# Feed-forward gate and up tiles as a 2x2 block product with seven products

## The chip, the cores and the metric

The kernel is one program on one core of a Trainium2 chip. Its time is device microseconds (us). Four engines compute: TensorE (PE; its weight loads are listed as PEld), VectorE (DVE), ScalarE (ACT) and GpSimd (POOL). SyncE (SP) issues all DMA transfers from one queue, in order. Every engine takes its own instructions in the order in which they stand in the program, and waits for others through semaphores.

## The reference, cut to what matters

The reference is an encoder of two layers (DEPTH = 2) on one sequence of 512 tokens of 1024 features, in float32. In each layer four token mixers (retention, chunk attention, gated linear attention and S5, a diagonal state-space model) work on projections of x. Their outputs are gated and summed, projected by `w_out` and normalised. A SwiGLU feed-forward part follows:

```python
x = _layer_norm(DEEPNORM_ALPHA * x + mixed @ w_out[l], ln1_g[l], ln1_b[l])
ffn = (jax.nn.silu(x @ w_ffn_gate[l]) * (x @ w_ffn_up[l])) @ w_ffn_down[l]
x = _layer_norm(DEEPNORM_ALPHA * x + ffn, ln2_g[l], ln2_b[l])
```

`w_ffn_gate` and `w_ffn_up` are 1024 x 2816, `w_ffn_down` is 2816 x 1024; 2816 is 22 tiles of 128.

## The kernel before, in words

All large products are made in a split form. An operand is cut into a high part that TensorE takes exactly and the low rest, and each product is three matmuls: high by high, low by high, high by low (`three`). A weight tile comes from DRAM as `wr` (128 x 1024, that is 8 blocks of 128 x 128 along the 1024 features); ACT casts it to `wh`, DVE subtracts that to `wl`. x is kept transposed in `XH` and `XL`.

A layer goes through four stages. (1) The mixers, a long stretch of small pieces that a planner (`Pace`, `run`) puts in order. (2) The `w_out` projection: `proj_ln` adds up 8 k-tiles in eight PSUM banks (`pj`), four token tiles t of 128 tokens by two halves of 512 features, then normalises each token tile (`layer_norm`). Its `rest` transposes the token tile (`tp`), scales it and writes it split into `XH` and `XL`; its `rows` scales it in rows, with 16 GpSimd operations in all, for the residual of the next projection. (3) Gate and up: for each of the 22 tiles f, two products `pg` (gate, then up) of 128 features by 512 tokens, each 8 blocks by 3 matmuls of 512 columns; ACT takes the silu, DVE multiplies to `fs`, and `fs` is split into `gh` and `gl` for the last stage. The first three products are made in two token halves of 256 columns (`gemm_ts`), so that TensorE has work while the token tiles t = 2 and 3 are normalised. (4) The down projection: `proj_ln` with 22 k-tiles of 24 matmuls. The first 18 go in the order of k, the last four by token tile.

One more thing runs beside stage 3 of layer 0, on GpSimd and DVE: the S5 constants of layer 1 (`s5_constants(1)`, tiles `s5w`, `ea`, `eb`), and from them eight tables (`s5_table`, tiles `er`, `ei`, `et`), which are stored in DRAM (`esp`) for the mixers of layer 1:

```python
if l + 1 < L and f == 0:
    s5c = s5_constants(l + 1)
if l + 1 < L and f % 2 == 0 and 4 <= f < 20:
    j = f // 2 - 2
    for i, x in enumerate(s5_table(j, s5c[3])):
        SP.dma_start(esp[j, i], x)
```

The order within an engine is the order of emission, moved by a scheduler that follows what is due. Tiles live in pools of 2 KB slots (53 general ones, 7 for `sg`, 8 for `acc`); a new tile waits until all that read or wrote its slot's last tile are done. The names in `order` and in the trace are the tile names; numbers behind them are single buffers.

Of the kernel before, what the change touches and what calls it, by code (L numbers as in the profile page):

```python
# [38 lines left out]
# 2 KB slots of SBUF per partition: in general, gates on hold, sums over branches  # L39
BUFS = {"a": 53, "sg": 7, "acc": 8}  # L40
# [92 lines left out]
def trunk_kernel(ctx: ExitStack, tc: tile.TileContext, xn, xt, wt, w2, wbr, wo, wgu, wdn,  # L133
# [12 lines left out]
    ap_ = pool("ap", 53)  # L146
# [9 lines left out]

    def slot(s, dt=F32, tag="a"):
        n = nm(s)
        return ap_.tile([P, 512], dt, tag=tag, name=n, bufs=BUFS[tag])

# [20 lines left out]

    def three(pairs):
# [44 lines left out]
        # theta * 2^k, reduced by multiples of 2 pi (exact products of short parts)  # L227
# [39 lines left out]
        # powers of exp(i theta), by doubling  # L267
# [22 lines left out]
    def s5_table(j, tabs):  # L290
        """exp(i theta n), n = 0..511, of a state tile"""
# [13 lines left out]
    # ------------------------------------------------------------- weight streams  # L305
# [17 lines left out]
    def wload_s(src):  # L323
        """the same into slots, in halves"""
# [10 lines left out]
    def gemm_t(src, s, late=None):  # L335
        """[128 features, 512 tokens] = (weight tile)^T x^T, in PSUM"""
# [17 lines left out]
    def gemm_n(srcs, width, pre=None, late=None):  # L354
        """four [128 tokens, width] = x (weight columns), in PSUM"""
# [24 lines left out]
    # ---------------------------------------------------------------- layer norm  # L380
    def layer_norm(l, w_, xh, pss, gt, bt, t, last):
        """x = LN(ALPHA x + psum) of one token tile, in place, the scale and shift left
        out; returns what is to be emitted later: x^T, split, and the scale and shift in rows"""
# [9 lines left out]
        power = G.tensor_tensor(rs, ve, mhalf, ALU.pow)  # L393
# [44 lines left out]
        return rest, rows, power  # L438

    def proj_ln(l, w_, lh, ll, nk, wsrc, kl, ks, xh, gt, bt, last):  # L440
        """x = LN(ALPHA x + a w): a^T split in lh/ll (nk k-tiles), w streamed by rows;
        returns what is left to do for the last token tile"""
# [20 lines left out]
        for t in range(4):  # L463
# [3 lines left out]
            todo.append(layer_norm(l, w_, xh[t], pss[t], gt, bt, t, last))  # L467
            if t > 0 and not last:
                todo[t - 1][0]()

        def rows():
            with tc.issue_after(todo[3][2].ins):
                for x in todo:
                    x[1]()

        return todo[3][0], rows
# [758 lines left out]
```

## Time and profile before

| | before |
|---|---|
| median of 3 runs | 1728.72 us (1725.3, 1728.72, 1729.99) |
| span of the profiled execution | 1727.3 us |
| TensorE busy, of the span | 1667.3 us, 97% |
| VectorE / ScalarE / GpSimd busy | 1000.5 / 621.2 / 347.6 us |
| gate and up, layer 0 (501.5 to 754.1) | 252.6 us |
| down projection, layer 0 (754.1 to 878.0) | 123.9 us |
| gate and up, layer 1 (1345 to 1600) | 255.0 us |

The profile is of one execution; the page gives its span, 1727.3 us, and no other time of that execution, which lies 1.4 us under the median of the runs. A stage's row in the view by windows gives the length of the window and then each engine's busy time and instructions. TensorE's records overlap (a matmul's end is modelled), so how fast it goes is read from the distance of the starts.

### The profile page before, as it was taken

The page shows a single profiled execution, that of the slowest core. Times are in us where ns is not written, and L with a number is a line of the kernel's source. Part 1 is how long each engine was busy: PE and PEld are TensorE (multiplying, and loading weights), DVE is VectorE, ACT ScalarE, POOL GpSimd, SP SyncE. Part 2 cuts the span into 40 slices and gives each one's busy share as a digit, 9 for nine tenths or more (in the row PEclk, how much of TensorE's full clock was granted, in tenths as well). Part 3 has the DMA queues.
Part 4 walks back from the last instruction along what each step waited for, and adds up shares of the span by engine and source line. Part 5 has one row for each costly group of instructions (what it writes and reads, how often), then busy time and mean ns, then how long its engine had stood idle before and what let it go on. Part 6 is the DMA issues. An engine that isn't in the chain of part 4 may idle for free. (4 is left out here: it accounts for less than half of the span.)

```text
span 1727.3 us, 19511 instructions
## 1 busy us (share of the span) xinstructions
PE 1667.3 (97%) x7468; PEld 1348.2 (78%) x7468; DVE 1000.5 (58%) x1473; ACT 621.2 (36%) x1012; POOL 347.6 (20%) x363
## 2 busy tenths in 40 slices
PE   8999998889999999999999999999999999999997
PEld 6778786667887888888887788877778888888886
DVE  4667579888577533322374765799875733333225
ACT  4454542233343322221253545433343532222112
POOL 0601025550038921000051000122200600000002
PEclk9998999899999999999999999999999999999999
DMA  6532212222423333322316433133424323322322
GB/s 198 174 108 77 85 61 93 81 88 91 145 94 98 122 122 122 110 98 97 110 61 235 130 99 95 62 119 122 135 80 158 104 92 98 98 87 97 98 98 73
DMA packets 66173, 186.41 MB, mean 108 GB/s; under 512 B 7136, under 2 KB 7328, under 8 KB 66080
## 3 DMA queue, kind: packets, MB, share of 16 engines
q1 hardware_dynamic: 66080, 185.17, 32.8%
q8 instruction: 59, 0.97, 0.2%
q14 instruction: 34, 0.28, 0.0%
HBM read 170.46 MB, written 14.68 MB: 107 GB/s over the span
## 5 line engine op out<-in xcount | busy, mean ns | idle before, releaser
L121 DVE TENSOR_TENSOR wl<-wr,wh 128x1024 fp32r<-128x1024 f32 (+2 forms) x250 | 316.8, 1268 | 537.3 <-PE pg L121 267.7
L121 ACT CAST wh<-wr 128x1024 fp32r<-128x1024 f32 (+2 forms) x250 | 257.5, 1031 | 554.2 <-PE pg L121 240.7
L121 PE MATMUL pg<-XH,wh 128*128 128x512 f32 (+1 forms) x1264 | 316.0, 391 | 1.8 <-DVE fs L121 1.8
L121 PE MATMUL pg<-XL,wh 128*128 128x512 f32 (+1 forms) x1264 | 314.1, 389 | 2.5 <-DVE XL L121 2.5
L121 PE MATMUL pg<-XH,wl 128*128 128x512 f32 (+1 forms) x1264 | 311.2, 388 | 0.0
L121 PEld LDWEIGHTS pg<-XL,wh 128*128 128x128 f32 x1264 | 233.1, 189 | 57.1 <-DVE XL L121 3.3
L121 PEld LDWEIGHTS pg<-XH,wh 128*128 128x128 f32 x1264 | 232.4, 190 | 55.6 <-issue 3.0
L121 PEld LDWEIGHTS pg<-XH,wl 128*128 128x128 f32 x1264 | 232.7, 189 | 54.0
L121 POOL TENSOR_TENSOR rs<-ve,ct 128x1 f32<-128x1 f32 x16 | 10.9, 682 | 727.5 <-DVE ve L121 727.5
L121 PE MATMUL pj<-wl,gh 128*128 128x512 f32 x320 | 102.9, 395 | 0.0
L121 PE MATMUL pj<-wh,gh 128*128 128x512 f32 x320 | 102.7, 394 | 0.0
L121 PE MATMUL pj<-wh,gl 128*128 128x512 f32 x320 | 102.6, 394 | 0.0
L121 POOL TENSOR_TENSOR acc<-acc,sg 128x512 f32<-128x512 f32 x32 | 55.3, 1732 | 170.6 <-DVE sg L121 170.6
L121 ACT CAST gh<-fs 128x512 fp32r<-128x512 f32 x44 | 27.3, 621 | 126.0 <-DVE fs L121 126.0
L121 PEld LDWEIGHTS pj<-wh,gh 128*128 128x128 f32 x320 | 60.3, 188 | 13.8
L121 PEld LDWEIGHTS pj<-wl,gh 128*128 128x128 f32 x320 | 60.3, 188 | 13.7
L121 PEld LDWEIGHTS pj<-wh,gl 128*128 128x128 f32 x320 | 60.3, 188 | 13.4
L121 PE MATMUL gn<-wh,XH 128*128 128x400 f32 (+1 forms) x128 | 49.8, 389 | 5.7 <-ACT XH L121 5.7
L121 ACT ACTIVATE sg<-pg,hb 128x512 f32<-128x512 f32 x64 | 43.9, 686 | 23.4 <-PE pg L121 23.1
L121 DVE TENSOR_TENSOR gl<-fs,gh 128x512 fp32r<-128x512 f32 x44 | 35.1, 797 | 29.7 <-ACT gh L121 29.7
L121 POOL TENSOR_TENSOR hr<-hv,ct 128x8 f32<-128x8 f32 x8 | 13.5, 1687 | 189.6 <-DVE hv L121 189.6
L121 PE MATMUL pb<-brh,bwh 128*128 128x512 f32 x128 | 51.6, 403 | 0.0
(320 smaller groups left out, 2562.2 us busy)
## 6 DMA issues: line engine op xcount, KB each, us to landing
wr<-in_wt SPq DMA_DIRECT2D x90, 512.0 KB
wr<-in_wgu SPq DMA_DIRECT2D x88, 512.0 KB
wr<-in_wdn SPq DMA_DIRECT2D x44, 512.0 KB
bwr<-in_wbr SPq DMA_DIRECT2D x32, 256.0 KB
wr<-in_wo SPq DMA_DIRECT2D x16, 512.0 KB
skr<-spr SPq DMA_DIRECT2D x32, 192.0 KB
wr<-in_w2b SPq DMA_DIRECT2D x8, 400.0 KB
wr<-in_w2a SPq DMA_DIRECT2D x8, 256.0 KB
```

What stands on the lines that cost most here:

```text
L121: r = fn(out, *a, **kw)
```

## The change

Per tile f, gate and up are now one 2 x 2 block product. The two block rows are gate and up; the inner dimension is cut into features 0-511 and 512-1023 (`a11, a12` of the gate's weights, `a21, a22` of up's), and the tokens into 0-255 and 256-511 (`b11, b21`, `b12, b22`). Seven block products stand for eight, each 4 blocks x 3 matmuls of 256 columns. They need sums of weights (`s1` to `s4`, four GpSimd additions of 128 x 512 per tile, each then split by ACT and DVE like a weight), sums of x blocks (`t1` to `t4`, made once per layer in `block_sums`), and five additions from PSUM on DVE per tile. The weight loads of gate (`wr`) and up (`wu`) stay two DMAs per tile.

Around it: `fs` times `fy` (`g`) is kept unsplit until the down projection, which splits it itself (`aph`, `apl`). The normalised rows are stored in DRAM (`xsp`) in `rest`, loaded again in `residual`, and scaled there by the 16 GpSimd operations that `rows` had, ahead of the next projection. SBUF's general slots are laid out anew for each phase: 37 + 7 + 8 for the mixers and the `w_out` projection, then 22 held tiles `g` with the feed-forward's own slots, then 30 for the down projection. The S5 constants and tables of layer 1 are emitted in the k loop of layer 0's down projection.

```diff
+MIXERS = {"a": 37, "sg": 7, "acc": 8}
+HELD = {"g": 22}
+FFN = {"wu": 2, "ws": 5, "wk": 14, "po": 7}
+DOWN = {"a": 30}
...
+    def block_sums(sums, t, xf):
+        raw, parts = sums
+        raw.append(xf)
+        if t < 2:
+            return
+        e = G if t == 2 else V
+        (b11, b21), (b12, b22) = raw[t - 2], xf
+        t1, t2, t3, t4 = (slot("bs", tag="a" if t == 2 else "g") for _ in range(4))
+        cols = slice(P * (t - 2), P * (t - 2) + P)
+        for i, (o, a, b) in enumerate(((t1, b12, b11), (t2, b22, t1), (t3, b22, b12), (t4, b21, t2))):
+            e.tensor_tensor(o, a, b, ALU.subtract)
+            h, l_ = (x[:, :, cols] for x in parts[i])
+            split(h, l_, o.rearrange("p (k c) -> p k c", c=P))
+
+    def residual(l, which, src, scaled):
+        xh = [[kept(f"x{h}") if t == 3 else slot("x") for h in range(2)] for t in range(4)]
+        gb = None if scaled else ln_params(l, which)
+        for t in range(4):
             for h in range(2):
-                G.tensor_tensor(xh[h], xh[h], gt[h], ALU.mult)
-                G.tensor_tensor(xh[h], xh[h], bt[h], ALU.add)
...
+                SP.dma_start(xh[t][h], src[P * t:P * t + P, 512 * h:512 * h + 512])
+                if gb:
+                    G.tensor_tensor(xh[t][h], xh[t][h], gb[0][h], ALU.mult)
+                    G.tensor_tensor(xh[t][h], xh[t][h], gb[1][h], ALU.add)
+        return xh
...
         for k in range(nk):
             ws[k] = (wload_s(wsrc[k]) if k >= nk - ks else
                      [halved(x) for x in wload(wsrc[k])])
+            if not isinstance(a[k], tuple):
+                a[k] = split_slots("ap", a[k])
+            if also:
+                also(k)
...
+        def weights(f):
+            rg, ru = wp.tile([P, 1024], F32, tag="wr", name=nm("wr"), bufs=2), slot("wu", tag="wu")
+            h, l_ = (wp.tile([P, 1024], F32R, tag=t, name=nm(t)) for t in ("wh", "wl"))
+            SP.dma_start(rg, wgu[l, 2 * f])
+            SP.dma_start(ru, wgu[l, 2 * f + 1])
+            split(h, l_, rg)
+            a11, a12, a21, a22 = rg[:, 0:512], rg[:, 512:1024], ru[:, 0:512], ru[:, 512:1024]
+            w = {1: (h[:, 0:512], l_[:, 0:512]), 2: (h[:, 512:1024], l_[:, 512:1024])}
+            s1, s2, s3, s4 = (slot("ws", tag="ws") for _ in range(4))
+            G.tensor_tensor(s1, a21, a22, ALU.add)
+            G.tensor_tensor(s2, s1, a11, ALU.subtract)
+            G.tensor_tensor(s3, a11, a21, ALU.subtract)
+            G.tensor_tensor(s4, a12, s2, ALU.subtract)
+            for n, x in ((6, s2), (5, s1), (7, s3), (3, s4), (4, a22)):
+                w[n] = split_slots("wk", x, ("wk", "wk"))
+            return w
...
+        def tile_of(w, pa, u, s):
+            pb, pc = mx_ps("fb")[:, 0:256], mm_ps("fc")[:, 0:256]
+            y = slot("fy", tag="po")
+            p1, u2, p15 = u[:, 0:256], u[:, 256:512], y[:, 256:512]
+            product(pb, w[6], t2, True)
+            V.tensor_tensor(u2, pb, p1, ALU.add)
+            product(pc, w[5], t1, True)
+            V.tensor_tensor(p15, pc, p1, ALU.add)
+            if s is None:
+                s = head2(w, pa)
+            product(pb, w[7], t3, False)
+            V.tensor_tensor(p15, pb, p15, ALU.add)
+            product(pc, w[3], b22, False)
+            V.tensor_tensor(s[:, 256:512], pc, u2, ALU.add)
+            A.activation(s[:, 256:512], s[:, 256:512], AF.Silu)
+            product(pb, w[4], t4, False)
+            V.tensor_tensor(y[:, 0:256], pb, p1, ALU.add)
+            return s, y
...
+    def tables(k):
+        if k == 0:
+            s5c_[0] = s5_constants(1)
+        elif k % 2 == 0 and k <= 16:
+            for i, x in enumerate(s5_table(k // 2 - 1, s5c_[0][3])):
+                SP.dma_start(esp[k // 2 - 1, i], x)
...
+        phase("ff", FFN)
+        gs = ffn(l, parts, rest)
+        close()
+        phase("dn", DOWN)
+        xh = residual(l, 0, xsp, False)
+        gt, bt = ln_params(l, 1) if l == L - 1 else (None, None)
+        rest = proj_ln(l, 1, gs, NF, wdn[l], 4, 2, xh, gt, bt, l == L - 1,
+                       also=tables if l + 1 < L else None)
```

Here is how this stands in the queues at three places. First TensorE at the entry of layer 0's gate and up, before the change; `tp` are the transposes of token tile 2 (`x_3916`, `x_3917`) and 3 (`x_3918`, `x_3919`):

```order
1057 L121 MATMUL tp_4292<-ct,x_3916 128x128 x4
1058 L121 MATMUL tp_4293<-ct,x_3917 128x128 x4
1059 L121 MATMUL pg_4342<-XH,wh_4325 128x256 x8
1060 L121 MATMUL pg_4342<-XL,wh_4325 128x256 x8
1061 L121 MATMUL pg_4342<-XH,wl_4326 128x256 x8
1062 L121 MATMUL pg_4343<-XH,wh_4331 128x256 x8
1063 L121 MATMUL pg_4343<-XL,wh_4331 128x256 x8
1064 L121 MATMUL pg_4343<-XH,wl_4332 128x256 x8
1065 L121 MATMUL tp_4393<-ct,x_3918 128x128 x4
1066 L121 MATMUL tp_4394<-ct,x_3919 128x128 x4
1067 L121 MATMUL pg_4344<-XH,wh_4337 128x256 x8
```

The same place after the change; `fa` are the block products of the gate's own weights, `fc_4577` is the first product with a weight sum (`wkh_4361` is the high part of `s1`):

```order
1035 L126 MATMUL tp_4296<-ct,x_3916 128x128 x4
1036 L126 MATMUL tp_4297<-ct,x_3917 128x128 x4
1037 L126 MATMUL fa_4377<-XH,wh_4343 128x256 x4
1038 L126 MATMUL fa_4377<-XL,wh_4343 128x256 x4
1039 L126 MATMUL fa_4377<-XH,wl_4344 128x256 x4
1040 L126 MATMUL tp_4394<-ct,x_3918 128x128 x4
1041 L126 MATMUL tp_4395<-ct,x_3919 128x128 x4
1042 L126 MATMUL fa_4468<-XH,wh_4434 128x256 x4
1043 L126 MATMUL fa_4468<-XL,wh_4434 128x256 x4
1044 L126 MATMUL fa_4468<-XH,wl_4435 128x256 x4
1045 L126 MATMUL fa_4377<-XH,wh_4343 128x256 x4
1051 L126 MATMUL fc_4577<-XH,wkh_4361 128x256 x4
```

Between the transposes of token tiles 2 and 3 stood 48 matmuls of 256 columns, and 12 stand there now; behind the third token tile come 36 more before the first product with a sum.

Second, SP's queue in the same stretch, after the change: the eight stores of the rows and two loads of them stand ahead of the first load of up's weights (`wu_4342`).

```order
150 L126 DMA xsp<-x_3918 128x512
151 L126 DMA xsp<-x_3919 128x512
152 L126 DMA x_7383<-xsp 128x512
153 L126 DMA x_7384<-xsp 128x512
154 L126 DMA wu_4342<-in_wgu 128x1024
155 L126 DMA wu_4433<-in_wgu 128x1024
```

Before, no store of rows stood in this stretch, and no load of them.

Third, SP's queue in layer 0's down projection. Before, it held nothing but the loads of `wr` for one k-tile after the other:

```order
212 L121 DMA wr_6263<-in_wdn 128x1024
213 L121 DMA wr_6293<-in_wdn 128x1024
214 L121 DMA wr_6323<-in_wdn 128x1024
215 L121 DMA wr_6353<-in_wdn 128x1024
216 L121 DMA wr_6383<-in_wdn 128x1024
217 L121 DMA wr_6413<-in_wdn 128x1024
```

After, each load from the sixth k-tile on (`wr_7734`) to the twelfth (`wr_7974`) but the first stands behind stores of the tables, each of which waits for GpSimd to have made it:

```order
223 L126 DMA wr_7848<-in_wdn 128x1024
224 L126 DMA esp<-ei_7939 128x512
225 L126 DMA esp<-er_8018 128x512
226 L126 DMA esp<-ei_8019 128x512
227 L126 DMA wr_7894<-in_wdn 128x1024
228 L126 DMA esp<-er_8098 128x512
229 L126 DMA esp<-ei_8099 128x512
230 L126 DMA wr_7928<-in_wdn 128x1024
231 L126 DMA esp<-er_8178 128x512
232 L126 DMA wr_7974<-in_wdn 128x1024
```

The 16 stores stood among the weight loads of gate and up before; they stand among those of the down projection now, and the last weight load behind one is the twelfth k-tile's.

## Rows read from the trace of the kernel before

**Rows 1.** The page: busy time, share; a costly group (busy, mean ns | idle).

```profile
PE 1667.3 (97%) x7468; PEld 1348.2 (78%) x7468; DVE 1000.5 (58%) x1473; ACT 621.2 (36%) x1012; POOL 347.6 (20%) x363
...
L121 ACT CAST wh<-wr 128x1024 fp32r<-128x1024 f32 (+2 forms) x250 | 257.5, 1031 | 554.2 <-PE pg L121 240.7
```

**Rows 2.** By windows: length; busy (x instructions) of PE, PEld, DVE, ACT, POOL; clock, DMA, GB/s.

```profile
501.50:754.10 252.60, 248.49 (x1140) 201.76 (x1139) 116.79 (x139) 79.99 (x106) 108.44 (x123) 1.00 0.36 115
754.10:878.00 123.90, 123.90 (x542) 100.65 (x541) 42.13 (x54) 30.60 (x45) 1.66 (x3) 1.00 0.28 89
...
1345.00:1600.00 255.00, 252.72 (x1163) 206.52 (x1162) 100.55 (x106) 81.72 (x106) 27.17 (x17) 1.00 0.30 98
```

**Rows 3.** Timeline, TensorE, gate and up: start, us, engine, line, operation, count.

```profile
502.53 1.07 PE L121 MATMUL pg<-XL,wh 128*128 128x256 f32 x8
...
506.16 1.07 PE L121 MATMUL pg<-XH,wl 128*128 128x256 f32 x8
...
744.76 2.03 PE L121 MATMUL pg<-XL,wh 128*128 128x512 f32 x8
746.63 2.03 PE L121 MATMUL pg<-XH,wl 128*128 128x512 f32 x8
```

**Rows 4.** Timeline, VectorE, layer 0's gate and up.

```profile
504.82 0.69 DVE L121 TENSOR_TENSOR XL<-xf,XH 128x512 fp32r<-128x512 f32 x1
...
529.79 1.22 DVE L121 TENSOR_TENSOR wl<-wr,wh 128x1024 fp32r<-128x1024 f32 x1
...
558.35 2.03 DVE L121 TENSOR_TENSOR wl<-wr,wh 128x1024 fp32r<-128x1024 f32 x1 [2.25 <-PE pg L121]
...
565.91 0.68 DVE L121 TENSOR_TENSOR fs<-fs,pg 128x512 f32<-128x512 f32 x1
```

**Rows 5.** Groups by form, VectorE: busy, mean ns of one.

```profile
L121 DVE SCALAR_TENSOR_TENSOR pp<-as,nb 128x256 f32<-128x256 f32 x24 | 9.8, 414 | 0.6 <-PE as L121 0.6
```

**Rows 6.** Timeline, GpSimd, layer 0's gate and up.

```profile
517.54 3.53 POOL L121 TENSOR_TENSOR x<-x,lg 128x512 f32<-128x512 f32 x2
...
526.05 2.52 POOL L121 TENSOR_TENSOR x<-x,lb 128x512 f32<-128x512 f32 x2
...
534.78 0.20 POOL L121 TENSOR_TENSOR ea<-eb,s5w 128x8 f32<-128x8 f32 x1 [6.05 <-ACT s5w L121]
...
556.23 1.05 POOL L121 TENSOR_TENSOR er<-ea,eb 128x512 f32<-128x512 f32 x1
...
558.25 1.04 POOL L121 TENSOR_TENSOR ei<-ea,eb 128x512 f32<-128x512 f32 x1
559.26 2.26 POOL L121 TENSOR_TENSOR er<-er,et 128x512 f32<-128x512 f32 x1
...
584.98 1.28 POOL L121 TENSOR_TENSOR er<-er,et 128x512 f32<-128x512 f32 x1
...
605.36 1.28 POOL L121 TENSOR_TENSOR ei<-ei,et 128x512 f32<-128x512 f32 x1
```

**Rows 7.** Timeline, TensorE, transposes of token tile 3; idle time before in brackets.

```profile
507.52 0.66 PE L121 MATMUL tp<-ct,x 128*128 128x128 f32 x4 [0.29 <-DVE x L121]
508.92 0.66 PE L121 MATMUL tp<-ct,x 128*128 128x128 f32 x4 [0.75 <-DVE x L121]
```

**Rows 8.** Timeline, VectorE beside GpSimd's row operations.

```profile
505.95 2.91 DVE L121 TENSOR_SCALAR x<-x,mv,rs 128x512 f32<-128x512 f32 x2 [0.44 <-POOL rs L121]
...
523.64 5.37 DVE L121 TENSOR_SCALAR s5w<-s5w 128x72 f32<-128x72 f32 x5
```

**Rows 9.** Timeline, SyncE's queue at the entry of gate and up.

```profile
503.54 15.48 SPq L121 DMA_DIRECT2D wr<-in_wgu  x2
```

**Rows 10.** DMA from 495 to 560 us: GB/s in 40 slices.

```profile
GB/s 0 0 0 0 124 306 305 393 168 10 0 0 0 0 0 222 101 0 0 0 0 0 40 272 176 164 3 78 245 35 287 219 103 103 219 0 20 303 0 0
```

**Rows 11.** By windows, around a wait in layer 0's mixers.

```profile
325.00:330.00 5.00, 1.26 (x3) 1.09 (x4) 4.94 (x6) 2.75 (x5) 2.04 (x2) 0.71 0.35 105
330.00:335.00 5.00, 5.00 (x15) 3.89 (x15) 1.20 (x3) 1.19 (x2) 5.00 (x6) 0.61 0.00 0
```

More of the change, by code (lines that the diff above doesn't have):

```diff
@@ L155, in nm, with phase, close, kept @@
         return f"{s}{uid[0]}"
-    def slot(s, dt=F32, tag="a"):
+    phases = []
+    def phase(name, tags):
+        st = ExitStack()
+        phases.append((st, st.enter_context(tc.tile_pool(
+            name=nm(name), bufs=1, reuse_waits="tile")), tags))
+    def close():
+        phases.pop()[0].close()
+    def slot(s, dt=F32, tag="a"):
+        p, tags = next(x[1:] for x in phases if tag in x[2])
+        return p.tile([P, WIDE.get(tag, 512)], dt, tag=tag, name=nm(s), bufs=tags[tag])
+    def kept(s):
+        return lp.tile([P, 512], F32, tag=s, name=nm(s))
+    def pair(s):
         n = nm(s)
-        return ap_.tile([P, 512], dt, tag=tag, name=n, bufs=BUFS[tag])
+        return bp.tile([P, 1024], F32R, tag="b", name=n, bufs=PAIRS)
     def mm_ps(s):
@@ L378, in gemm_n, with layer_norm @@
         return pss
-    def layer_norm(l, w_, xh, pss, gt, bt, t, last):
+    def layer_norm(l, w_, xh, pss, gt, bt, t, last, sums):
         st = sm.tile([P, 2, 6], F32, tag="st", name=nm("st"))
@@ L392, in layer_norm @@
         V.tensor_scalar(ve, mv[:, 1:2], EPS, None, ALU.add)
[L393 removed]
+        G.tensor_tensor(rs, ve, mhalf, ALU.pow)
         if last and t == 3:
@@ L412, in rest @@
         def rest():
+            for h in range(2):
+                SP.dma_start(xsp[P * t:P * t + P, 512 * h:512 * h + 512], xh[h])
             tp = [mx_ps("tp") for _ in range(2)]
-            xf = [slot("xf") for _ in range(2)]
+            xf = [kept(f"xf{h}") if sums is not None and t == 1 else
+                  slot("xf", tag="g" if sums is not None and t == 3 else "a") for h in range(2)]
             for h in range(2):
@@ L466, in proj_ln @@
                     prod(k, t, (h,))
-            todo.append(layer_norm(l, w_, xh[t], pss[t], gt, bt, t, last))
+            todo.append(layer_norm(l, w_, xh[t], pss[t], gt, bt, t, last, sums))
             if t > 0 and not last:
[L469 to L476, printed above, removed]
+                todo[t - 1]()
+        return todo[3]
     def ln_params(l, which):
@@ L998, in trunk_kernel, with ffn, product, head @@
     xsp = dr.tile([S, D], F32, name="xsp")
+    PRE = 3
+    def ffn(l, parts, rest):
+        X = lambda k0, c0: [[x[:, k0 + k, c0:c0 + 256] for k in range(4)] for x in (XH, XL)]
+        b11, b21, b22 = X(0, 0), X(4, 0), X(4, 256)
+        t1, t2, t3, t4 = ([[x[:, k, :] for k in range(4)] for x in p] for p in parts)
+        def weights(f):
[14 more added lines that the diff above has]
+            return w
+        def product(ps, w, x, first):
+            n = 0
+            for a, b in three((w, x)):
+                for k in range(4):
+                    T.matmul(ps, a[:, P * k:P * k + P], b[k], start=first and n == 0,
+                             stop=n == 11, skip_group_check=True)
+                    n += 1
+        def head(w):
+            pa = mx_ps("fa")[:, 0:256]
+            u = slot("fu", tag="po")
+            product(pa, w[1], b11, True)
+            A.copy(u[:, 0:256], pa)
+            return pa, u
+        def head2(w, pa):
+            product(pa, w[2], b21, False)
+            s = slot("fs", tag="po")
+            A.activation(s[:, 0:256], pa, AF.Silu)
+            return s
+        def tile_of(w, pa, u, s):
[16 more added lines that the diff above has]
+            return s, y
+        ws, hs, ss, gs = {}, {}, {}, []
+        for f in range(PRE):
+            ws[f] = weights(f)
+            hs[f] = head(ws[f])
+            if f == 0:
+                rest()
+            if f:
+                ss[f - 1] = head2(ws[f - 1], hs[f - 1][0])
+        ss[PRE - 1] = head2(ws[PRE - 1], hs[PRE - 1][0])
+        for f in range(NF):
+            if f >= PRE:
+                ws[f] = weights(f)
+                hs[f] = head(ws[f])
+            s, y = tile_of(ws.pop(f), *hs.pop(f), ss.pop(f, None))
+            g = slot("g", tag="g")
+            V.tensor_tensor(g, s, y, ALU.mult)
+            gs.append(g)
+        return gs
@@ L1062, in trunk_kernel @@
         g_gate = gate_stream(l, (1, 0, 2, 3), brs, mix)
-        run(g_gate, attention(l, aq, ak, va, brs[1]), ret(), gl(), s5(l, s5c, uspr, brs[3]))
-        xh = [[slot("x") for _ in range(2)] for _ in range(4)]
-        for t in range(4):
-            for h in range(2):
-                src = xn if l == 0 else xsp
-                SP.dma_start(xh[t][h], src[P * t:P * t + P, 512 * h:512 * h + 512])
-        gt, bt = ln_params(l, 0)
-        rest, rows = proj_ln(l, 0, [m[0] for m in mix], [m[1] for m in mix], 8, wo[l], 4, 2, xh, gt, bt, False)
@@ L1094, in trunk_kernel @@
-        rest, rows = proj_ln(l, 1, ghs, gls, NF, wdn[l], 4, 2, xh, gt, bt, l == L - 1)
+        run(g_gate, attention(l, aq, ak, va, brs[1]), ret(), gl(), s5(l, s5c_[0], uspr, brs[3]))
+        xh = residual(l - 1, 1, xn if l == 0 else xsp, l == 0)
+        parts = [[x[:, 0:4, 256:512] for x in (XH, XL)]]
+        for _ in range(3):
+            parts.append([pair(x).rearrange("p (k c) -> p k c", c=256) for x in ("bh", "bl")])
+        rest = proj_ln(l, 0, mix, 8, wo[l], 4, 2, xh, None, None, False, ([], parts))
```

69 lines of the change are left out of this document (29 added, 40 removed).

## The prediction

> **What bounds the kernel now.** I read the busy line first, then the view by windows, then the timelines of the stages that the change touches. TensorE is busy for 97% of the span [rows 1], and in the three stages in question it is the bound by itself: in layer 0's gate and up it has 248.49 of 252.60 us, in its down projection 123.90 of 123.90, in layer 1's gate and up 252.72 of 255.00. In the first of these GpSimd has 108.44 us of work, in the down projection 1.66 [rows 2]. So matmul time that goes there is gained one for one until another engine comes last, and GpSimd is free through the whole down projection.
>
> **The change part by part.**
>
> *Matmuls of gate and up.* Eight matmuls of 512 columns start 1.87 us apart, 233.4 ns each; a tile of 48 takes 11.2 us. Those of 256 columns, each with its own weight load, also stand in the trace: from 502.53 to 506.16 are 32, 113.4 ns each [rows 3]. A tile has 84 of them now: 9.53 us. For 22 tiles that is 209.6 instead of 246.5 us, 36.9 us less per layer if nothing else is late.
>
> The Trainium skill, "TensorE: Matmul & The Clock Gate", section "Back-to-back issue gap", speaks against this: the spacing in a stream is set by weight load and matmul together, 81 ns with 128 columns and 131 with 512. Between these, 256 columns come to some 98 ns, an estimate, and 84 of them would take 8.2 us against 6.3 for 48 long ones: 1.9 us more per tile, 85 us slower in all. The trace does not bear this out, 113.4 against 233.4 ns; the sum goes by the rows.
>
> *VectorE and GpSimd per tile.* DVE has `wl` (1.22 us alone), five more low parts and the product `g` (0.69 each by the low part of that size) [rows 4], and five additions from PSUM of 128 x 256 (0.41, nearest row [rows 5]): 7.4 us. GpSimd has four sums at 1.28 us (its addition alone, at 584.98): 5.1 us [rows 6]. They do not run freely beside each other. At 558.35 `wl` took 2.03 instead of 1.22 while GpSimd finished `ei`, and GpSimd's next addition, at 559.26, took 2.26 instead of 1.28; with one operand in PSUM DVE was not slowed (`fs` at 565.91, 0.68) [rows 4, 6]. So `wl`, the five low parts, `g` and the four sums (5.4 + 5.1 = 10.5 us) take turns. The one collision shown took 2.26 us where the two alone take 2.50, a ratio of 0.90, which makes 9.5 us of 9.53. It just fits. The tight chain is in the tile's second half: the cast of the next gate weights waits for the eighth matmul of the fourth product (5.0 us into the tile), takes 1.03 [rows 1], then `wl` 1.22, then an addition of 0.41, without which the seventh product (8.17 us into the tile) may not start: 2.7 us of 3.2. GpSimd's next `s1` is released just ahead of `wl`; one collision of 0.8 us overruns this by 0.3 to 0.4. I take 9.9 us per tile, 217.8 per layer; the ends are 9.53 (TensorE alone) and 12.5 (all 7.4 and 5.1 one after the other).
>
> *Entry of gate and up.* Before, the stage had 252.6 - 246.5 = 6.1 us beyond its matmuls. Token tile 3's transposes came at 507.5 and 508.9 [rows 7], held by DVE's scaling of x, 2.91 us beside GpSimd [rows 8]; the block sums of token tile 2 now stand on GpSimd where the row operations stood, so these times stay. TensorE reaches them with 12 matmuls (1.4 us) instead of 48 (5.4): it waits from 503 to 507.5, and again until 508.9. The 36 next matmuls last until about 513.5. Then comes the first product with a sum. Its `wu` load stands behind the stores of x and their reloads, and its slot waits until DVE has split GpSimd's last block sum: four sums from 503 with the normalisation's power between end at 509.5, cast and low part near 511.4. A load takes some 3 us (issued at 519.02 [rows 9], its bytes moved by 522.6 [rows 10]), so `s1` starts near 514.5 and `s4` ends near 519.6. ACT casts `s2` ahead of `s1`, and the next gate weights behind `s4`: the product starts near 519.5, the one behind it near 522.5. By 524 TensorE has done six products (8.2 us) and the transposes (0.8) in 22.5 us. With some 1.5 us for the clock, which was at 0.61 in the 5 us after a wait of 3.7 [rows 11], I take 15 us per layer, ends 6 (as before) and 20.
>
> Stage: 217.8 + 15 = 232.8 us. Gain 19.8 us in layer 0, 22.2 in layer 1, together 42.
>
> *Entry of the down projection.* The first k-tile's low part waits for the last `g` (two operations of 0.69): 1.4 us per layer that were hidden before, in layer 0 part of what follows.
>
> *Layer 0's down projection.* Here GpSimd's work comes out of cover. Counted from the last `g`: the slots of `lb` wait for it, its loads take 3 us; 14 of the 16 row operations follow, 1.26 us each alone and 1.77 beside DVE [rows 6]: 17.6 to 24.8, I take 19. DVE's constants (22 small operations, up to 1.07 us each beside GpSimd [rows 8]) end about then. GpSimd's part of the constants took from 534.78 to 556.23, 21.4 us; I take 20. Then the tables: six from 556.23 to 606.64, 8.4 us each; from single durations without turns 4 x 1.05 + 2 x 1.28 = 6.8 [rows 6]. DVE has one `wl` and one low part per k-tile here, less than there; I take 7.8, 62 for eight. That is 3 + 19 + 20 + 62 = 104 us. SP's weight loads from the seventh k-tile on stand behind stores that wait for tables, and on ACT the cast of the eleventh k-tile's weights stands behind the split of a later `g` whose slot is the last table's. So the eleventh starts 2 us later (a cast, a low part), at 106; what TensorE did before is of no matter, since the first ten k-tiles (56 us) end long before. Twelve k-tiles of 24 x 233.4 ns, 67.2 us, are left: 173 after the last `g`, 174.5 after the last matmul of the stage before, against 123.9 [rows 2]. Loss 50.5 us. Ends: 3 + 17.6 + 15 + 54 + 2 + 67.2 + 1.4 = 160 (36 lost; 15 for constants by leaving out their turns), and 3 + 24.8 + 21.4 + 67.2 + 2 + 67.2 + 1.4 = 187 (63 lost).
>
> *Mixers, `w_out` projection, layer boundary.* The general slots go from 53 to 37 with six pairs beside; TensorE's order there hardly moves. The 16 row operations at layer 1's start go and come back ahead of its `w_out` projection, hidden by TensorE's eight k-tiles unless a slot is late. A late slot costs a wait like that at 325, 3.7 us and 2 us of clock [rows 11]. I take 3 us, ends -3 and +17.
>
> *Sum* against the span of 1727.3: -42 + 1.4 + 50.5 + 3 = +12.9, 1740.2. The median of the runs lies 1.4 us above that span: 1741.6, rounded to 1741.
>
> **The rivals.**
>
> *TensorE sets the pace everywhere.* For it: the turns come to 9.5 us, no more than the matmuls. A tile of 9.6 and an entry of 8 make the stage 219.2, gains of 33.4 and 35.8; with a loss of 40 in the down projection the sum is -69 + 1.4 + 40 = -28: 1701. Against it: the entry's loads and casts in one file.
>
> *The tables do not hold the down projection.* If slots and loads ran far enough ahead, GpSimd's 104 us would fit into 123.9 and some 5 us would be lost: -42 + 1.4 + 5 + 3 = -33, 1696. Against it: the queue order, where weight loads stand behind the stores.
>
> *The turns of DVE and GpSimd bound the tile* (ends on the other side of these two). It decides from a tile of 10.2 us on. At 10.8, a little over the full 10.5 without any overlap, the stage takes 253, so nothing is gained: -2 + 1.4 + 50.5 + 3 = +53, 1782. For it: both queues are strict and the sums wait for the low parts of the tile before. Beside it stands a rule of the Trainium skill ("SBUF — State Buffer", section "Who interferes with whom"): a VectorE instruction with two SBUF inputs and a GpSimd one that reads SBUF exclude each other for the whole instruction. By this rule the tile would take 10.5 us; the trace agrees that they exclude each other, and shows 0.90 of the sum.
>
> *The mixers lose by fewer slots*: three late slots, +17 instead of 3: 1755. Against it: the order.
>
> **How the numbers follow.** Forecast 0.45 (own range 1722 to 1760), TensorE's pace 0.18, tables hidden 0.08, turns 0.20, mixers 0.09. A difference under 0.3% (5 us) can hardly be told from none here. Faster: the 0.26 of the two first rivals and 0.05 of the forecast, 0.31; I add 0.01 for parts that I have not seen. Within: 0.12, from the forecast's lower part. Slower: the rest, 0.56. The range, 1698 to 1782, reaches over most of the faster rivals and to the turns' price, and leaves out their far ends.
>
> **What would show it.** Gate and up: starts of eight 256-column matmuls 0.91 us apart, a tile in 9.5 to 10.2 us, DVE's low parts often near 1.3 us. Entry: TensorE idle at 503, and again ahead of the first `fc`, until about 520. Down projection of layer 0: GpSimd busy for about 100 us, TensorE waiting from the sixth k-tile on for casts that follow GpSimd, layer 1 starting 25 to 35 us later than at 878. It is wrong if that stage takes under 150 us, or if a tile takes over 10.2 us.

## The result, and the profile after

The changed kernel takes 1882.3 us (1878.3 to 2068.2 in four runs), the kernel before 1729.4: a ratio of 1.087, interval 1.084 to 1.090. (The longest of the four was a disturbed run and is not in the ratio.) The forecast was 1741, the range 1698 to 1782. The direction was right, the size was not. The profiled execution has a span of 1877.3 us, 150.0 more than before.

The page after, busy time and share of the span [rows 1]:

```profile
PE 1667.9 (89%) x8908; PEld 1410.6 (75%) x8908; DVE 1275.0 (68%) x1889; ACT 717.1 (38%) x1288; POOL 642.0 (34%) x547
```

TensorE's busy time is what it was, in 8908 instead of 7468 matmuls; its share fell from 97 to 89%. VectorE has 275 us more, GpSimd 294. To see where the time went, the span is cut at landmarks that both traces have: the transposes of token tile 2 in each `proj_ln` of a `w_out` projection or a down projection, and the first matmul of each down projection. Lengths in us; the later rows are the experiments below.

| | mixers, `w_out`, layer 0 | gate, up, layer 0 | down, layer 0 | mixers, `w_out`, layer 1 | gate, up, layer 1 | down, end | span |
|---|---|---|---|---|---|---|---|
| before | 500.7 | 253.4 | 124.8 | 466.8 | 251.0 | 130.6 | 1727.3 |
| after | 515.6 | 284.2 | 178.0 | 473.3 | 284.4 | 141.8 | 1877.3 |
| e1 loads in order | 516.9 | 268.1 | 176.8 | 478.0 | 259.4 | 142.5 | 1841.8 |
| e2 tables in layer 1 | 516.6 | 284.4 | 135.4 | 506.5 | 285.4 | 142.5 | 1870.8 |
| e4 no weight sums | 512.8 | 237.9 | 177.4 | 477.1 | 236.0 | 141.5 | 1782.6 |
| e5 = e1, sums on VectorE | 516.4 | 243.4 | 178.3 | 476.9 | 240.6 | 143.2 | 1798.7 |
| e8 sums on VectorE only | 515.9 | 246.8 | 177.0 | 476.8 | 243.0 | 143.2 | 1802.6 |
| e6 residual on VectorE | 513.4 | 285.1 | 173.0 | 475.4 | 287.0 | 145.6 | 1879.5 |
| e7 = e5 and e6 | 517.0 | 243.0 | 172.4 | 475.1 | 241.7 | 146.2 | 1795.5 |
| e9 no residual rows | 514.9 | 285.8 | 158.6 | 476.3 | 286.2 | 132.2 | 1854.1 |
| e10 = e5, late residual | 518.3 | 243.9 | 173.7 | 474.8 | 242.3 | 132.1 | 1784.9 |
| e11 = e10, other store queue | 516.2 | 244.1 | 174.1 | 475.2 | 240.8 | 132.2 | 1782.7 |
| b1 before, 45 slots | 505.0 | 254.9 | 122.8 | 470.2 | 251.3 | 132.0 | 1736.3 |
| b2 before, 41 slots | 517.8 | 252.9 | 124.8 | 477.6 | 251.0 | 130.5 | 1754.5 |

After less before: +14.9, +30.9, +53.3, +6.5, +33.4, +11.2. Layer 0's mixers have the same code in all versions of the changed kernel and took 512.8 to 518.3 us, so a few us in that column say nothing. The view by windows shows the four stages of the feed-forward parts after (columns as in [rows 2]):

```profile
515.64:799.86 284.22, 238.08 (x1866) 231.91 (x1864) 214.65 (x289) 118.59 (x223) 153.94 (x93) 0.95 0.26 91
799.86:977.87 178.01, 138.59 (x544) 108.84 (x545) 86.24 (x114) 41.97 (x67) 99.56 (x125) 0.87 0.32 108
1451.16:1735.54 284.38, 237.08 (x1865) 230.92 (x1863) 216.32 (x289) 119.11 (x224) 154.79 (x93) 0.95 0.27 91
1735.54:1877.30 141.76, 124.02 (x528) 99.89 (x528) 63.98 (x82) 35.45 (x48) 33.59 (x26) 0.95 0.33 105
```

In gate and up TensorE now stands still for 46 us of 284; no engine is full there. That suggests a loop of waits, and the timeline of one steady tile shows one (start, us, engine, line, operation, count, idle time before in brackets):

```profile
644.77 2.12 POOL L126 TENSOR_TENSOR ws<-wu 128x512 f32<-128x512 f32 x1 [4.73 <-DMA wu<-in_wgu]
...
649.83 1.75 POOL L126 TENSOR_TENSOR ws<-wr,ws 128x512 f32<-128x512 f32 x1
651.61 0.33 SPq L126 DMA_DIRECT2D wr<-in_wgu  x1
652.03 0.38 SPq L126 DMA_DIRECT2D wu<-in_wgu  x1
655.17 1.05 ACT L126 CAST wh<-wr 128x1024 fp32r<-128x1024 f32 x1 [2.81 <-DMA wr<-in_wgu]
656.25 1.23 DVE L126 TENSOR_TENSOR wl<-wr,wh 128x1024 fp32r<-128x1024 f32 x1 [1.66 <-ACT wh L126]
656.47 2.15 POOL L126 TENSOR_TENSOR ws<-wu 128x512 f32<-128x512 f32 x1 [4.88 <-DMA wu<-in_wgu]
657.39 0.42 DVE L126 TENSOR_TENSOR fy<-fb,fy 128x256 f32<-128x256 f32 x1
657.87 0.51 PE L126 MATMUL fb<-bh,wkh 128*128 128x256 f32 x2 [1.44 <-DVE fy L126]
...
661.55 1.76 POOL L126 TENSOR_TENSOR ws<-wr,ws 128x512 f32<-128x512 f32 x1
663.34 0.33 SPq L126 DMA_DIRECT2D wr<-in_wgu  x1
...
668.20 2.12 POOL L126 TENSOR_TENSOR ws<-wu 128x512 f32<-128x512 f32 x1 [4.89 <-DMA wu<-in_wgu]
```

Go round it. `wr` has two buffers, so the load of a tile's `wr` waits until the last sum of the tile two before it (`ws<-wr,ws`, ends 651.58) has read the old one, and starts at 651.61. The scheduler has put the load of the tile before, `wu`, behind it on SyncE; it had nothing to wait for, but starts at 652.03. Its bytes release GpSimd's first sum at 656.47, 4.44 us later. The four sums last until 663.31, 6.84 us, and only then may the next `wr` start, at 663.34. That is 11.73 us per tile, and the distance of the `ws<-wu` rows is 11.70 and 11.73. TensorE feels it further on: `wr` lands late, so do `wh`, `wl` and, in VectorE's queue behind `wl`, the addition `fy` that the last product of `fb` waits for: 1.44 us here.

The entry of layer 0's gate and up, timeline:

```profile
500.91 21.98 SPq L126 DMA_DIRECT2D xsp<-x  x8
526.66 0.81 SPq L126 DMA_DIRECT2D wu<-in_wgu  x2
...
530.34 1.83 POOL L126 TENSOR_TENSOR ws<-wu 128x512 f32<-128x512 f32 x1 [6.66 <-DMA wu<-in_wgu]
535.48 1.75 POOL L126 TENSOR_TENSOR ws<-wr,ws 128x512 f32<-128x512 f32 x1
...
535.58 1.22 PE L126 MATMUL fc<-XH,wkh 128*128 128x256 f32 x4 [6.52 <-ACT wkh L126]
539.51 1.23 PE L126 MATMUL fc<-XH,wkl 128*128 128x256 f32 x4 [1.85 <-DVE wkl L126]
541.83 1.22 PE L126 MATMUL fa<-XH,wh 128*128 128x256 f32 x4 [1.10 <-ACT wh L126]
```

The shape is the forecast's: stores of x ahead of `wu`, then sums, then the first `fc`. But the waits go on, one behind the other, and TensorE is slow in between. Windows of the same stretch (columns as above):

```profile
530.00:540.00 10.00, 2.57 (x10) 2.27 (x11) 9.86 (x8) 4.61 (x9) 9.50 (x6) 0.65 0.24 86
540.00:553.00 13.00, 9.96 (x51) 9.17 (x51) 10.20 (x11) 6.29 (x11) 6.23 (x5) 0.61 0.25 84
553.00:566.00 13.00, 9.44 (x70) 9.04 (x71) 11.23 (x14) 4.25 (x7) 8.07 (x6) 0.91 0.21 82
566.00:580.00 14.00, 11.33 (x77) 11.14 (x77) 12.30 (x16) 4.89 (x8) 9.04 (x6) 0.84 0.22 75
580.00:600.00 20.00, 19.70 (x163) 19.30 (x162) 16.93 (x24) 9.51 (x17) 9.49 (x6) 1.00 0.30 107
```

Of its two levels, 1.2 and 2.4 GHz, TensorE has mostly the lower one in the first 23 us (granted clock 0.65 and 0.61), with a wait of 6.5 us at their start, mostly the upper one after that (0.91, 0.84), and only the upper one from 580 on (1.00). VectorE is busy for 9.86 of the first 10 us, with eight instructions.

Layer 0's down projection, timeline:

```profile
803.09 2.60 POOL L126 TENSOR_TENSOR x<-x,lg 128x512 f32<-128x512 f32 x2 [21.34 <-DMA lg<-in_lng]
...
824.30 0.20 POOL L126 TENSOR_TENSOR ea<-eb,s5w 128x8 f32<-128x8 f32 x1
...
842.36 1.05 POOL L126 TENSOR_TENSOR er<-ea,eb 128x512 f32<-128x512 f32 x1
849.41 0.62 ACT L126 CAST aph<-g 128x512 fp32r<-128x512 f32 x1 [20.93 <-POOL ei L126]
851.03 1.22 PE L126 MATMUL pj<-wh,aph 128*128 128x512 f32 x2 [7.74 <-ACT wh L126]
...
902.24 1.22 PE L126 MATMUL pj<-wl,aph 128*128 128x512 f32 x2 [3.63 <-DVE wl L126]
904.33 1.27 POOL L126 TENSOR_TENSOR ei<-ei,et 128x512 f32<-128x512 f32 x1
```

Row operations take 21 us, constants 18, eight tables 63: GpSimd runs from 803.1 to 905.6, and the split of g (`aph`) follows its tables, because each takes the place of an earlier table's tile. The eleventh k-tile starts at 909.8, 4.2 us behind the last table. Its own weights are cast by 907.2, but TensorE is then still at the tenth, whose `wl` (the wait of 3.63 us) stood in VectorE's queue behind splits of g that waited for tables. Up to this last link it is the chain that the prediction counted.

In layer 1 there are no tables, and yet the end is 11.2 us longer. One wait makes 7.7 of it:

```profile
1757.34 0.62 ACT L126 CAST aph<-g 128x512 fp32r<-128x512 f32 x1 [18.20 <-POOL x L126]
...
1759.78 0.62 ACT L126 CAST aph<-g 128x512 fp32r<-128x512 f32 x1 [1.82 <-POOL x L126]
...
1761.39 1.22 PE L126 MATMUL pj<-wh,aph 128*128 128x512 f32 x2 [7.67 <-ACT wh L126]
```

ScalarE's casts of g wait for slots that the residual's row operations hold, and the cast of the weights stands behind them.

### The profile page after: what moved, and what is told of

It reads as the page before. It is cut to its first block, busy times and chain, and to the rows that moved or that the text cites. A ratio compares the mean times of both kernels' runs of the same rounds, so it can differ in the third digit from the quotient of the medians.

```text
span 1877.3 us, 23758 instructions
## 1 busy us (share of the span) xinstructions
PE 1667.9 (89%) x8908; PEld 1410.6 (75%) x8908; DVE 1275.0 (68%) x1889; ACT 717.1 (38%) x1288; POOL 642.0 (34%) x547
## 5 line engine op out<-in xcount | busy, mean ns | idle before, releaser
L126 DVE TENSOR_TENSOR wkl<-ws,wkh 128x512 fp32r<-128x512 f32 x176 | 177.2, 1008 | 60.0 <-ACT wkh L126 54.4
L126 ACT CAST wkh<-ws 128x512 fp32r<-128x512 f32 x176 | 108.4, 617 | 168.9 <-POOL ws L126 121.9
L126 PE MATMUL pg<-XH,wh 128*128 128x512 f32 x512 | 136.4, 404 | 2.6 <-DVE sg L126 2.6
L126 PE MATMUL pj<-wh,aph 128*128 128x512 f32 x320 | 108.5, 414 | 31.0 <-ACT wh L126 22.3
L126 PE MATMUL pg<-XL,wh 128*128 128x512 f32 x512 | 135.7, 398 | 0.0
L126 PE MATMUL pg<-XH,wl 128*128 128x512 f32 x512 | 132.1, 396 | 0.0
L126 PE MATMUL pj<-wl,aph 128*128 128x512 f32 x320 | 108.1, 412 | 11.8 <-DVE wl L126 11.8
L126 PEld LDWEIGHTS pg<-XH,wh 128*128 128x128 f32 x512 | 98.0, 193 | 26.7 <-DVE sg L126 3.2
L126 PEld LDWEIGHTS pg<-XL,wh 128*128 128x128 f32 x512 | 95.7, 189 | 22.2
L126 PEld LDWEIGHTS pg<-XH,wl 128*128 128x128 f32 x512 | 95.5, 188 | 22.3
```

The costliest lines, as they stand in the source:

```text
L126: r = fn(out, *a, **kw)
```

## The experiments

All ratios are against the kernel before, run on the same chip beside them. Where no ratio is given there was one run.

**e1: the loop.** Theory: SyncE's order closes a loop. Rival: the turns of VectorE and GpSimd, or TensorE's pace. From the fourth tile on, the edit puts each `wr` load behind the `wu` load of the tile before.

```
+            with (tc.issue_after(wudma[0].ins) if f >= PRE else ExitStack()):
                 SP.dma_start(rg, wgu[l, 2 * f])
-            SP.dma_start(ru, wgu[l, 2 * f + 1])
+            wudma[0] = SP.dma_start(ru, wgu[l, 2 * f + 1])
```

> The change, with one edit: from the fourth tile f on, the load of a gate tile (wr) is queued on SP behind the load of the up tile (wu) of the tile before it; nothing else is changed. Theory 1 (a loop through SP's queue): in the changed kernel wu of a tile stands behind a wr that waits for the fourth sum of the tile before, so load (4.4 us) and four sums (6.8 us) follow each other and make the tile of 11.7 us; in order, wu is loaded ahead, GpSimd no longer waits for it, and the tile falls to 10.0 to 10.6 us (84 matmuls at 119 ns are 10.0), each gate and up stage from 284 to 250 to 260 us, the whole to 1815 to 1835 us. Theory 2 (turns of VectorE and GpSimd bound the tile): the turns stay, the tile stays at 11.2 to 11.7 us, the whole at 1870 to 1885 us.

1842.2 us, ratio 1.064 (1.060 to 1.068). The order of two loads gives back 16.1 and 25.0 us. That speaks against the rival, but it is less than the loop theory forecast (1815 to 1835). The mean tile from the first `g` to the last is 10.73 us in layer 0 and 10.33 in layer 1, the median 10.67 and 10.62. GpSimd still waits some 4 us for `wu`, but the loop no longer sets the tile. What is left shows in e1's timeline:

```profile
649.92 1.75 POOL L126 TENSOR_TENSOR ws<-wr,wu 128x512 f32<-128x512 f32 x1
...
650.43 2.33 DVE L126 TENSOR_TENSOR wl<-wr,wh 128x1024 fp32r<-128x1024 f32 x1
...
651.63 2.27 POOL L126 TENSOR_TENSOR ws<-wr,ws 128x512 f32<-128x512 f32 x1
...
652.68 0.41 DVE L126 TENSOR_TENSOR fy<-fb,fy 128x256 f32<-128x256 f32 x1
...
653.15 0.38 PE L126 MATMUL fb<-bh,wkh 128*128 128x256 f32 x1 [0.83 <-DVE fy L126]
```

`wl` takes 2.33 us beside GpSimd instead of 1.23, and `fy` stands behind it. This is the chain of which the prediction says: "The tight chain is in the tile's second half".

**e4: without the sums.** The four sums are left out (products use unsummed blocks); what is then left of a tile is TensorE, splits and additions.

```
-            G.tensor_tensor(s1, a21, a22, ALU.add)        (and s2, s3, s4)
+            s1, s2, s3, s4 = a21, a11, a11, a12
```

> The change without GpSimd's four weight sums per tile: the plain quarters of the weights are split and used in their place (this part of the computation is left out). Theory 1 (loop): without sums no wu is waited for, the tile is 10.0 to 10.2 us, the whole 1790 to 1820 us. Theory 2 (turns): the same tile, since no turns are left. It gives the floor of the tile, from which the run with loads in order shows what turns cost by themselves. If the tile stays over 10.8 us, the split work of VectorE or ScalarE bounds it and both are wrong.

1788.0 us, ratio 1.033 (1.029 to 1.037), 2 us below the range expected. Gate and up take 237.9 and 236.0 us, a steady tile 10.02. That is TensorE's own pace: its groups of four matmuls start 0.477 us apart, and a tile has 21. The changed kernel's timeline has the same distance where nothing is waited for (19 steps from the first of these rows to the last):

```profile
658.45 0.64 PE L126 MATMUL fb<-bl,wkh 128*128 128x256 f32 x4
...
667.51 0.64 PE L126 MATMUL fc<-XH,wkl 128*128 128x256 f32 x4
```

So GpSimd's sums, with all they cause, cost 46 and 48 us; and with no sums at all the entry is 237.9 - 22 x 10.02 = 17.5 us, where the forecast's 15 us included them.

**e5 and e8: the same sums on VectorE.** They tell apart how long VectorE's instructions are from how many it has. e5 is e1 with `G.tensor_tensor` replaced by `V.tensor_tensor` in the four sums; e8 has only that replacement.

```
-            G.tensor_tensor(s1, a21, a22, ALU.add)        (and s2, s3, s4)
+            V.tensor_tensor(s1, a21, a22, ALU.add)
```

> The loads in order, and the four sums of a tile on VectorE in place of GpSimd. Against the run with the loads in order alone (1842 us; its steady tile 10.73 us; 44 us from the stage's start to the first tile's g). Theory 1, the lengthened VectorE instructions are the rest of the tile: alone, VectorE has 4 x 0.68 + 5 x 0.68 + 1.23 + 5 x 0.41 + 0.68 = 10.1 us per tile, TensorE 10.0, so the tile is 10.1 to 10.5 us, wl takes 1.23 us again in place of 2.06 to 2.33, and the time is 1805 to 1830 us. Rival, what counts is how many instructions stand ahead of fy in VectorE's queue: with four more of them the tile is 11.0 to 11.5 us and the time 1848 to 1865 us.

> The changed kernel with the four sums on VectorE, the loads in the order they have in it. Theory 1, the loop through SyncE's queue is long because of GpSimd's 6.8 us for four sums: on VectorE they take 4 x 0.68 us within its other work, some 3.5 to 5.4 us from first to last, so the loop is 4.4 + 0.5 + 3.5 to 5.4 = 8.4 to 10.3 us, hardly longer than TensorE's 10.0: a tile of 10.0 to 10.5 us and 1798 to 1812 us in all. Rival, the order of the loads costs its microsecond per tile whatever makes the sums: tile 11.0 us, time 1835 to 1850 us.

e5: 1800.4 us, ratio 1.039 (1.037 to 1.041), 5 us below the range of its theory. e8: 1804.4 in one run, inside its theory's range. In layer 0 the median tile is 10.05 us in e5 and 10.17 in e8, where tiles reach 11.1. The row of `wl` in e5, and the window of layer 0's gate and up in e5 and then in e1:

```profile
645.24 1.22 DVE L126 TENSOR_TENSOR wl<-wr,wh 128x1024 fp32r<-128x1024 f32 x1
```

```profile
516.41:759.77 243.36, 229.97 (x1865) 227.20 (x1863) 215.57 (x376) 123.52 (x223) 5.82 (x5) 0.97 0.33 106
516.85:784.99 268.14, 236.90 (x1865) 232.00 (x1864) 227.29 (x289) 124.32 (x223) 154.66 (x93) 0.95 0.28 96
```

In e5 VectorE does 87 instructions more than in e1, which has the same order of loads, and is busy for 11.7 us less, 215.6 instead of 227.3; in the changed kernel it was 214.7. So what it lost beside GpSimd's sums in e1 was more than it takes to do them itself. The Trainium skill says in "SBUF — State Buffer", section "Who interferes with whom", that a VectorE instruction with two SBUF inputs and a GpSimd one that reads SBUF contend for ports that they share, by an exclusive lock. The trace agrees: in the rows of e1, `wl` (1.22 us alone) ends 1.09 us after the sum that ran when it started, and the next sum (1.28 alone) ends 1.14 us after `wl`. With the sums on VectorE the order of the loads is worth 4 us in all (e8 against e5, spans), with the sums on GpSimd it was worth 35.5: the loop needs both the order and the long sums.

**e2: the tables back in layer 1.**

```
-            s5c_[0] = s5_constants(0)        (layer 0 only)
+        s5c_[0] = s5_constants(l)
...
-                       also=tables if l + 1 < L else None)
+                       also=None)
```

> The change, with the S5 constants and tables of layer 1 taken out of layer 0's down projection and made in layer 1's own mixers, as layer 0 makes its own (no stores to DRAM). Theory 1 (the tables hold the down projection): it falls from 178 us to what layer 1's takes over 124, some 9 us more: 132 to 136; layer 1's mixers get 60 to 80 us of GpSimd work beside TensorE and lose 5 to 25 us; the whole falls to 1842 to 1862 us. Theory 2 (the 16 row operations and the 30 slots hold it, the tables only fill the time): the down projection stays above 155 us and the whole above 1865.

1878.1 us, ratio 1.084 (1.080 to 1.087): missed. Layer 0's down projection falls by 42.6 us, as expected, and layer 1's mixers grow by 33.2, more than the 5 to 25 expected. So making the tables there costs 33.2 of the 42.6 us that it saves here; why it costs so much was not looked into. The 135.4 left are 10.6 over before, about as much as the end of layer 1, which has no tables either.

**e6, e9, e10: the residual's row operations.** e6 puts them on VectorE (`G.` becomes `V.` in `residual`), e7 joins e5 and e6. e9 leaves the residual's scale and shift out in the down projections. e10 is e5 with `residual` called at k-tile 18 of 22 in layer 0, behind the tables, and at 10 in layer 1.

```
-        xh = residual(l, 0, xsp, False)
+        xh = []                          (e10; filled at k-tile 18 or 10)
...
+            if k == (18 if l + 1 < L else 10):
+                xh.extend(residual(l, 0, xsp, False))
```

> The changed kernel, with the residual's scale and shift (16 row operations per layer) on VectorE in place of GpSimd. Theory 1, the down projection waits for GpSimd's queue: in layer 0 the constants start 21 us earlier and the last table ends 21 us earlier, so that stage takes 155 to 162 us in place of 178; in layer 1 the slots come free in time and the end takes 130 to 136 us in place of 142; in all 1848 to 1860 us. Rival, VectorE's turns are as scarce: 16 x 0.69 = 11 us more of it in each down projection make its splits late, and the time stays at 1872 to 1890 us.

> Loads in order, sums and residual's row operations on VectorE, together. If the three theories hold, the parts add: the time of the run with the sums on VectorE, less 20 to 28 us: 1780 to 1805 us, still above before's 1729 by mixers, entry and tables. If VectorE is the scarce one in the down projection, 1810 to 1840 us.

> The changed kernel without the scale and shift of the residual in the down projections: their 16 GpSimd operations per layer are left out. Theory 1, GpSimd's queue holds the down projections: in layer 1, where no tables are made, the end falls from 142 to 130 to 134 us (before 131); in layer 0 constants and tables come 21 us earlier and the stage falls from 178 to 155 to 162 us. Rival, the slots that loads and splits wait for are too few in any case (30 in place of 53): the end stays at 139 to 143 us, and layer 0 gains under 10 us.

> Sums on VectorE, loads in order, and the residual's loads and row operations emitted behind the tables (k-tile 18 in layer 0, 10 in layer 1) in place of ahead of everything in the down projection; nothing is left out. Theory 1, it is the row operations' place at the head of GpSimd's queue, and the slots that they keep, that cost what leaving them out gave back: layer 0's down projection 178 to 157 to 164 us, the end 143 to 130 to 135 us, in all 1766 to 1780 us, the shortest of the versions, still 35 us above before. Rival, the same 21 us of GpSimd come back at the stage's end, ahead of the layer norm: 1790 to 1803 us.

e6: 1879.2 us, ratio 1.084 (1.082 to 1.086); its theory failed, the rival held. In its timeline VectorE's row operations stand ahead of the first low parts and of VectorE's share of the constants, so TensorE and GpSimd wait for them:

```profile
812.54 1.22 PE L126 MATMUL pj<-wh,apl 128*128 128x512 f32 x2 [11.97 <-DVE apl L126]
...
819.53 1.02 POOL L126 TENSOR_TENSOR ea<-eb,s5w 128x8 f32<-128x8 f32 x1 [31.95 <-ACT s5w L126]
```

e7: 1795.8, ratio 1.036 (1.035 to 1.038): within its first range, but only 4.6 us below e5, not 20 to 28; the intervals of the two overlap.

e9, 1855.9 in one run, gave what its theory said: layer 0's stage 158.6, the end 132.2, with no wait left in layer 1 but the first. Its constants start at 805.6 instead of 824.3. So GpSimd's queue is what both stages wait for.

e10: 1785.2, ratio 1.030 (1.028 to 1.032), between the ranges of theory and rival. In layer 1 the end is 132.1 with nothing left out. In layer 0 it gives 4.6 us: there the row operations come after the tables and TensorE waits for them instead:

```profile
872.37 0.62 ACT L126 CAST aph<-g 128x512 fp32r<-128x512 f32 x1 [13.82 <-POOL x L126]
...
873.99 1.22 PE L126 MATMUL pj<-wh,aph 128*128 128x512 f32 x2 [7.07 <-ACT wh L126]
```

Theory and rival each hold in one layer: where GpSimd has 21 us of work the place decides, where it has 100 the sum does.

**e11: stores from GpSimd's queue.** It tests the prediction's picture of weight loads held behind the tables' stores on SyncE.

```
-                SP.dma_start(esp[k // 2 - 1, i], x)
+                nc.gpsimd.dma_start(esp[k // 2 - 1, i], x)
```

> The same, with the tables' stores issued from GpSimd's queue in place of SyncE's, so that no weight load of the down projection stands behind a store. Theory 1, SyncE's order makes the weights late: the waits of the projection for wh and wl go (each 2 to 6 us) and layer 0's stage is 10 to 25 us shorter than with the late residual alone. Rival, the casts of g wait for a table's slots whatever SyncE does, so the stage follows GpSimd's 8 x 7.5 us: less than 5 us of difference, or some microseconds longer by the issues on GpSimd.

1782.9 us, ratio 1.029 (1.028 to 1.031), the shortest of the versions, though not clear of e10. Layer 0's down projection takes 174.1 instead of 173.7: the queue order is not what holds it here. That it does not in the changed kernel either, where the row operations come first, was not tried by itself.

**b1 and b2: the kernel before with fewer slots.** `BUFS["a"]` of 53 becomes 45, and 41.

> The kernel before with 45 general slots instead of 53. Theory 1 (fewer slots make the mixers slower): layer 0's w_out projection starts 8 to 15 us later than at 454.8. Theory 2 (the planner's other order with paired tiles does it): it starts within 3 us of that. A deficit in later stages says nothing here.

> The kernel before with 41 general slots in place of 53 (45 slots gave +4.3 us in layer 0's mixers). Theory 1, the smaller store of slots is what the mixers lose in the changed kernel: layer 0's mixers and output projection take 509 to 516 us (before 500.7, changed 515.6). Rival, the changed order of the steps: 504 to 508 us.

1738.3 and 1756.3 us in one run each. b1 falls between the ranges of its two theories, b2 a little above that of its first. Layer 0's mixers and projection lose 4.3 and 17.1 us, layer 1's 3.4 and 10.8. The largest waits of TensorE from 60 to 515 us (us in total, times, longest), of the changed kernel and then of b2, are the same ones, while before's list begins with `sv`:

```profile
PE sy L126 <- ACT xrh L126: 8.9, 4, 4.1
PE sg L126 <- ACT swgh L126: 3.5, 1, 3.5
PE hn L126 <- DVE go L126: 3.5, 2, 1.8
```

```profile
PE sy L121 <- ACT xrh L121: 8.9, 4, 4.2
...
PE hn L121 <- DVE go L121: 3.5, 2, 1.8
PE sg L121 <- ACT swgh L121: 3.5, 1, 3.5
```

```profile
PE sv L121 <- DVE sbs L121: 11.2, 3, 5.0
```

So fewer slots alone, in the old order, make a loss of this size by the same waits. That they make all of it in the changed kernel follows from the likeness; no run gave the changed kernel its slots back.

No version beats the kernel before. e11 is 55.4 us over its span: gate and up -9.3 and -10.2, the mixers +15.5 and +8.4, layer 0's down projection +49.3, the end +1.6. To make the tables beside gate and up, where GpSimd is busy for only 5.82 of 243.36 us in e5, was not tried.

## Why the prediction was wrong, step by step

The span is 137 us over the forecast's 1740.2 (whose 1741.6 for the runs was rounded down to 1741). Gate and up make 106 of them (a gain of 42 forecast, a loss of 64 measured), the mixers 18, the end 10, layer 0's down projection 3. That the direction came out right is owed to layer 0's down projection alone: for gate and up the forecast had the wrong sign.

*Matmuls, 113.4 ns.* Slightly off. Groups of four matmuls start 0.47 to 0.48 us apart, 119 ns each, where groups of eight in before had 113.4 [rows 3]. A tile is 10.02 us of matmuls instead of 9.53.

*"I take 9.9 us per tile."* This is the step that failed: 11.72, or 40 us per layer, over the 10.2 that the prediction named as the sign of being wrong. Part is the turns, which it saw and made too small ("one collision of 0.8 us overruns this by 0.3 to 0.4"): the four sums take 6.84 instead of 5.1 us, and with the loads in order (e1), where `wl` takes up to 2.33, the median tile is 10.67, against 10.05 without collisions (e5). The other microsecond is the loop through SyncE, which it did not look for: it summed busy times and followed one chain within a tile, but not who releases `wr` and what stands behind that load. The trace of before could not show the loop; SyncE's order in the changed kernel, with `wr` of the next tile ahead of `wu`, could have. The two lie on top of one another: sums on VectorE end the turns and nearly all of the loop (e8).

*Entry, 15 us.* The mechanism was right, the size too small: 284.2 - 22 x 11.72 = 26.4 us. The first product with a sum came 19.9 us into the stage (forecast 18.0). What was missed lies behind it: sums and splits of the first three tiles stand one behind another and TensorE waits for them again and again. And its 43 matmuls between 535.6 and 550 ran at the lower clock level, 0.85 us per group of four instead of 0.48: some 4 us by these numbers (an estimate), where the forecast had 1.5. The entry is 17.5 us without the sums (e4) and 243.4 - 22 x 10.02 = 23 with them on VectorE (e5). Together with the tile this is 51.4 us of layer 0's stage, and 51.6 of layer 1's.

*Entry of the down projection and layer 0's down projection, +1.4 and 50.5 us.* Right: layer 1's entry has a wait of 1.14 us, and layer 0's stage is 53.3 longer. Row operations 21 (forecast 19), constants 18 (20), tables 63 (62), and the eleventh k-tile starts 110 us into the stage (forecast 107.4). Two of its reasons did not hold. Taking the weight loads from behind the stores made no difference (e11, with the row operations late). And what TensorE did before was not "of no matter": the tenth k-tile ends 2.6 us after the eleventh's weights are cast, and is what the eleventh waits for. By these 2 to 3 us the close agreement is luck.

*Layer 1's down projection.* Forecast with no loss beyond the 1.4 us of the entries: +11.2. The row operations that hold slots were counted in layer 0 and forgotten in layer 1, where e9 and e10 show them.

*Mixers, +3.* Mis-sized: +21.4 in the two layers together, over the upper end of +17. The rival "the mixers lose by fewer slots" was right about the mechanism, against the reason given for its low chance ("the order"): in the old order, too, fewer slots make the same waits (b2). The price was read too low as well: the "3.7 us" of [rows 11] is the part inside that window of a wait of 5.0, which is before's longest in the rows above.

*Rivals.* "Turns of DVE and GpSimd bound the tile", at 10.8, is nearly e1's tile of 10.67, so it describes what remains when the loop is cut; alone it explains 0.8 of the 1.8 us by which the tile exceeds 9.9. "TensorE's pace" is where e5 arrives, with a gain of 10 us per layer for gate and up instead of 33 to 36. "Tables hidden" was wrong.

## What to carry to other kernels

Where a change adds loads and long operations per tile, do not stop at busy times: for each load write down which instruction frees its buffer and what stands behind it in its queue, and follow that around to the same load of the next tile; the sum around the ring is a lower bound of the tile. An engine that looks free is worth nothing if its long instructions lengthen those of a neighbour that TensorE waits for: count both. Buffers that a change takes from another stage have a price there, which the old kernel with fewer buffers measures without the change.

## What was unexpected

VectorE took over the 88 sums of layer 0's gate and up (e5) and was busy for 0.9 us more than in the changed kernel and for 11.7 us less than in e1, while GpSimd lost 148 us of work. Matmuls of 256 columns started 119 ns apart in groups of four and 113.4 in groups of eight; why is open. Between 45 and 41 slots the mixers and projections of the kernel before lost 12.8 and 7.4 us, between 53 and 45 only 4.3 and 3.4.
